# RWKV inverse in 16 by 16 blocks with its off-diagonal blocks on TensorE, new step weights, casts with priority, and another order in a sum of squares

## The chip, the cores and the metric

The kernel runs on one core of one Trainium2 chip. The metric is the device time of one execution in microseconds: before the change the median of 3 runs is 1454.53 us (1451.75 to 1456.83).

## The reference

Two layers (DEPTH = 2) over 256 tokens of width 1024, all in float32. Each layer is a half-step SwiGLU network, a mixer of three parallel branches, and a second half-step SwiGLU network. The mixer's branches are differential attention, RWKV-7 and HGRN2, all fed by one projection `u @ w_in`. The part that matters here is the RWKV recurrence, per head (8 heads, 64 by 64 state), one token after another:

```python
s_kk  = state @ kk_t
state = state * w_t - s_kk (x) (kk_t * a_t) + v_t (x) k_t
out_t = state @ r_t
```

and the normalisation ahead of each sub-layer, `y = x * rsqrt(mean(x*x) + eps) * w`, which needs the sum of squares of the residual stream over its 1024 channels.

## The kernel before, in words

**Weights.** All matrix products run on TensorE with every weight and activation split in two parts (high and low, type fp32r), three matmuls for each product (`mm3`, lines 363 to 369; the token-major form is lines 953 to 955). A weight tile is 128 by 1024 and takes 24 matmuls of 256 columns or 12 of 512. `load` (line 1339) fetches it into `raw` by a DMA on SP's queue; `split` (line 371) makes the high part `wh` by a cast on ScalarE (line 372) and the low part `wl` by a subtraction on VectorE (line 373). There are 4 `raw`, 3 `wh` and 3 `wl` buffers, and the program loads two tiles ahead of the one it multiplies.

**The order of the work.** The weights of one layer are a list of items; `ORDER` (line 52) is the mixer's part of it. Before the products of an item, `advance` (line 283) gives the other work a credit (`BUDGET`: 1.5 to 2.4 for an item in the stretch in question) and lets the side tracks take steps until it is spent. A step is a piece of a Python generator up to its `yield`; the yielded number is its price, and a negative one also ends the track's turn for this item. Tracks in the mixer are R (RWKV), H (HGRN2, `levels`), A, S0 and S1 (attention). What is emitted this way is then put in order for each engine, when the program is built, by a planner that goes by priority (earlier emitted is higher) and by its own costs; `ahead(n)` (line 266) moves a piece n places up. The engines run their instructions strictly in the order so found.

**The RWKV inverse.** Tokens are cut in chunks of 64, 4 chunks and 8 heads, so 32 triangular 64 by 64 matrices A for each layer. `rwkv_rest` (line 774) needs the inverse of I + A for each. Before the change it is built from 32 by 32 blocks:

- The two diagonal blocks of each matrix (64 blocks) go through DRAM (`scr`, lines 783 and 789) into a layout with one block per partition; they lie there twice, so 128 partitions are filled.
- A loop over t = 1 to 15 (lines 798 to 803) finds row t of the inverse of both 16 by 16 diagonal blocks of each block by a product (line 800) and a reduction (line 802) on VectorE, over 2 t t elements.
- The off-diagonal 16 by 16 block is then two products and two reductions over 2048 elements, also on VectorE (lines 809, 812, 814, 817), with copies around them (lines 806, 807, 819, 820).
- The result goes back through DRAM (`scy`, lines 822 to 824 and 828) into `Ys`, where the rows of a matrix lie on the partitions.
- The off-diagonal 32 by 32 block is made on TensorE: a transpose on VectorE (line 838), 32 products of 32 by 32 for each half p (line 842), a copy on ScalarE (844), 32 more products (848) and a copy into `Ys` on VectorE (850). For a given p all products of a series use the same 32 by 32 tile of the array.

After it the scan over 4 chunks follows (lines 854 to 903), then the head's normalisation and output gate.

`levels` (line 996) waits until `M["inv"]` is set by `rwkv_rest`, and its buffers `hw`, `sc01` and `sc2` lie where `TM`, `NT` and `Y` lay. `a_open` (line 1115) drains R before the attention starts.

**The sum of squares.** For each of 8 residual tiles, `z_square` (line 412) squares on ScalarE; the first makes `acc`, tiles 1 to 6 are added to it on GpSimd (line 419), and the last stays in `sq`. `z_sums` (line 426) sums both over partitions by matmuls with ones into one PSUM tile, `acc` first. It is emitted with a priority 584 places up.

Of the kernel before, what the change touches and what calls it, by code (L numbers as in the profile page):

```python
# [63 lines left out]
def trunk(ctx: ExitStack, tc: tile.TileContext, A, out):  # L64
# [192 lines left out]
    NOW = {}  # L257
# [292 lines left out]
    scr = drp.tile([2, 2, 16, 32, 32], F32, name="scrA")  # L550
    scy = drp.tile([2, 2, 16, 32, 32], F32, name="scrY")
# [3 lines left out]
    def mixer(l):  # L555
# [218 lines left out]
        def rwkv_rest():  # L774
# [5 lines left out]
            for q in range(2):  # L780
                for p in range(2):
                    r0 = 64 * p + 32 * q
                    GP.dma_start(scr[q, p].rearrange("m s t -> s m t"),
                                 H[r0:r0 + 32, :, :, 32 * q:32 * q + 32].rearrange("s j c t -> s (j c) t"))
            NT = tile_([128, 32, 32], "NT", "r")
            Y = tile_([128, 32, 32], "Y", "k")
            TM = hp.tile([128, 2048], F32, name="TM", tag="ZH")
            for d in range(2):
                GP.dma_start(NT[64 * d:64 * d + 64], scr.rearrange("q p m s t -> (q p m) s t"))
            GP.memset(Y, 0.0)  # L790
            GP.memset(Y.rearrange("m a b -> m (a b)")[:, 0:1024:33], 1.0)
# [6 lines left out]
            for t in range(1, 16):  # L798
                tm = TM[:, 0:2 * t * t].rearrange("m (g j s) -> m g j s", g=2, j=t)
                V.tensor_tensor(tm, ap(Y, 0, [[528, 2], [32, t], [1, t]]), ap(NT, t, [[528, 2], [0, t], [32, t]]),  # L800
                                ALU.mult)
                V.tensor_reduce(ap(Y, t, [[528, 2], [32, t]]), tm, AX.X, ALU.add)  # L802
                yield 0.2 + 4 * t * t / 960.0
            Yh = tile_([128, 8, 16], "Yh", "rnt")
            PT = tile_([128, 8, 16], "PT", "rny")
            V.tensor_copy(Yh[0:64], Y[0:64, 0:8, 0:16])
            V.tensor_copy(Yh[64:128], Y[64:128, 8:16, 0:16])
            tm = TM.rearrange("m (j t s) -> m j t s", j=8, t=16)
            V.tensor_tensor(tm, Yh.unsqueeze(2).to_broadcast([128, 8, 16, 16]),  # L809
                            ap(NT, 16, [[0, 8], [1, 16], [32, 16]]), ALU.mult)  # L810
            yield 2.2
            V.tensor_reduce(PT, tm, AX.X, ALU.add)
            yield 2.2
            V.tensor_tensor(tm, PT.unsqueeze(2).to_broadcast([128, 8, 16, 16]),  # L814
                            ap(Y, 528, [[0, 8], [1, 16], [32, 16]]), ALU.mult)
            yield 2.2
            V.tensor_reduce(Yh, tm, AX.X, ALU.add)
            yield -2.2
            V.tensor_copy(Y[0:64, 0:8, 16:32], Yh[0:64])
            V.tensor_copy(Y[64:128, 8:16, 16:32], Yh[64:128])  # L820
            sm = scy.rearrange("q p m s t -> (q p m) s t")
            GP.dma_start(sm[:, 0:8], Y[0:64, 0:8])
            GP.dma_start(sm[:, 8:16], Y[64:128, 8:16])
            GP.dma_start(sm[:, 16:32], Y[0:64, 16:32])
            for q in range(2):
                for p in range(2):
                    r0 = 64 * p + 32 * q
                    GP.dma_start(Ys[r0:r0 + 32, :, 32 * q:32 * q + 32], scy[q, p].rearrange("m s t -> s m t"))
            M["inv"] = True
            yield 0.255  # L830

            Xa = tile_([128, 16, 32], "Xa")
            Tt = tile_([128, 16, 32], "Tt")
            p1 = psm([128, 16, 32])
            p2 = psm([128, 16, 32])
            hv = [(slice(64 * p, 64 * p + 32), slice(64 * p + 32, 64 * p + 64)) for p in range(2)]
            for a_, b_ in hv:
                V.transpose(Xa[a_], Ys[a_, :, 0:32])
            yield -1.2
            for p, (a_, b_) in enumerate(hv):  # L840
                for m in range(16):
                    PE.matmul(p1[b_, m], H[a_, m // 4, m % 4, 32:64], Xa[a_, m], start=True, stop=True,
                              tile_position=(64 * p, 64 * p + 32))
                SC.copy(Tt[b_], p1[b_])
            yield -0.2
            for p, (a_, b_) in enumerate(hv):
                for m in range(16):
                    PE.matmul(p2[a_, m], Tt[b_, m], Ys[b_, m, 32:64], start=True, stop=True,
                              tile_position=(64 * p + 32, 64 * p))
# [489 lines left out]
    def load(i):  # L1339
# [5 lines left out]
        split(wh, wl, raw)  # L1345
# [125 lines left out]
```

## Time and profile before

| | before |
|---|---|
| median of 3 runs | 1454.53 us |
| the profiled execution's own time | 1448.06 us |
| its span, first to last instruction | 1446.4 us |
| TensorE busy (matmuls) | 1397.5 us, 97% |
| VectorE busy | 1185.8 us, 82% |
| ScalarE busy | 804.4 us, 56% |
| GpSimd busy | 149.0 us, 10% |

Busy time is the union of an engine's instructions. Matmuls are pipelined, so the number of matmuls that a stretch holds says more of TensorE's pace than its busy share does. The mixers lie at about 220 to 560 us (layer 0) and 925 to 1260 us (layer 1).

### The profile page before, as it was taken

How to read it: one execution, taken by the hardware profiler on the slowest of the kernel's cores; microseconds unless marked ns; L12 is line 12 of the kernel's file. 1: busy time of each engine (PE TensorE's matmuls, PEld its weight loads, DVE VectorE, ACT ScalarE, POOL GpSimd, SP SyncE). 2: the span in 40 equal slices, each digit the busy share in tenths (PEclk: the TensorE clock that was granted, in tenths of full speed). 3: DMA queues.
4: the chain of work that ended last, by engine and by line, in shares of the span. 5: the costliest groups of instructions: out<-in, count | busy, mean ns of one | idle time of the engine just before them, and what ended most of it. 6: DMA issues, size and time to landing. Idle time of an engine off the chain costs nothing. (4 is left out here: it accounts for less than half of the span.)

```text
span 1446.4 us, 31230 instructions
## 1 busy us (share of the span) xinstructions
PE 1397.5 (97%) x12424; PEld 1325.0 (92%) x12424; DVE 1185.8 (82%) x2216; ACT 804.4 (56%) x1375; POOL 149.0 (10%) x251
## 2 busy tenths in 40 slices
PE   4999999999899999999999999999989999999998
PEld 2899999998778999999999999999877889999998
DVE  5899988869779999888879888787797787886553
ACT  3565457874255646554555554588534664565542
POOL 6100010031310021000100000100322001100000
PEclk9999999999799999999999999999999999999999
DMA  9679985445416657899878998644552235665664
GB/s 334 247 267 359 341 303 167 148 155 163 137 61 191 203 190 265 298 330 319 297 255 292 353 347 294 194 141 142 180 162 83 88 129 175 198 220 194 193 197 124
DMA packets 90212, 315.99 MB, mean 218 GB/s; under 512 B 10577, under 2 KB 13009, under 8 KB 90066
## 3 DMA queue, kind: packets, MB, share of 16 engines
q1 hardware_dynamic: 86690, 308.32, 63.0%
q0 software_dynamic: 1600, 4.20, 1.2%
q8 instruction: 97, 1.59, 0.4%
q10 hardware_dynamic: 1776, 1.48, 0.3%
q14 instruction: 49, 0.40, 0.1%
HBM read 311.86 MB, written 2.10 MB: 217 GB/s over the span
## 5 line engine op out<-in xcount | busy, mean ns | idle before, releaser
L372 ACT CAST wh<-raw 128x1024 fp32r<-128x1024 f32 (+1 forms) x440 | 455.9, 1036 | 427.4 <-PE psd L369 241.5
L373 DVE TENSOR_TENSOR wl<-raw,wh 128x1024 fp32r<-128x1024 f32 (+1 forms) x440 | 537.2, 1222 | 109.1 <-ACT wh L372 106.2
L369 PE MATMUL psd<-uh,wl 128*128 128x256 f32 x1664 | 227.5, 278 | 6.2 <-DVE wl L373 6.2
L369 PE MATMUL psd<-uh,wh 128*128 128x256 f32 x1664 | 230.8, 280 | 0.0
L369 PE MATMUL psd<-ul,wh 128*128 128x256 f32 x1664 | 226.6, 278 | 0.0
L369 PEld LDWEIGHTS psd<-uh,wl 128*128 128x128 f32 x1664 | 206.0, 188 | 7.9 <-DVE wl L373 7.4
L369 PEld LDWEIGHTS psd<-uh,wh 128*128 128x128 f32 x1664 | 207.2, 188 | 5.0 <-issue 2.6
L369 PEld LDWEIGHTS psd<-ul,wh 128*128 128x128 f32 x1664 | 206.0, 188 | 0.4
L321 DVE SCALAR_TENSOR_TENSOR mw<-mw,cbc 128x1024 f32<-128x1024 f32 x134 | 168.0, 1256 | 0.0
L369 PE MATMUL psd<-hl,wh 128*128 128x256 f32 x704 | 96.0, 277 | 0.0
L369 PE MATMUL psd<-hh,wl 128*128 128x256 f32 x704 | 95.9, 277 | 0.0
L369 PE MATMUL psd<-hh,wh 128*128 128x256 f32 x704 | 95.5, 276 | 0.0
L419 POOL TENSOR_TENSOR acc<-acc,sq 128x256 f32<-128x256 f32 x36 | 31.4, 873 | 573.2 <-ACT sq L417 572.9
L369 PEld LDWEIGHTS psd<-hh,wl 128*128 128x128 f32 x704 | 87.2, 188 | 0.0
L369 PEld LDWEIGHTS psd<-hl,wh 128*128 128x128 f32 x704 | 87.2, 188 | 0.0
L369 PEld LDWEIGHTS psd<-hh,wh 128*128 128x128 f32 x704 | 87.0, 188 | 0.0
L954 PE MATMUL psd<-wl,uh 128*128 128x512 f32 x160 | 66.9, 418 | 3.9 <-DVE wl L373 3.8
L955 PE MATMUL psd<-wh,ul 128*128 128x512 f32 x160 | 67.7, 423 | 0.0
L953 PE MATMUL psd<-wh,uh 128*128 128x512 f32 x160 | 66.4, 416 | 0.0
L369 PE MATMUL psd<-zh,wh 128*128 128x258 f32 x448 | 65.2, 286 | 0.0
L369 PE MATMUL psd<-zh,wl 128*128 128x258 f32 x448 | 64.9, 283 | 0.0
L369 PE MATMUL psd<-zl,wh 128*128 128x258 f32 x448 | 64.0, 283 | 0.0
(430 smaller groups left out, 2032.0 us busy)
## 6 DMA issues: line engine op xcount, KB each, us to landing
raw<-in_gu SPq DMA_DIRECT2D x176, 512.0 KB, 4.7
mw<-in_modw SPq DMA_DIRECT2D x134, 512.0 KB, 5.4
raw<-in_wfm SPq DMA_DIRECT2D x94, 512.0 KB, 3.3
raw<-in_dn SPq DMA_DIRECT2D x64, 512.0 KB, 4.6
raw<-in_wtm SPq DMA_DIRECT2D x40, 512.0 KB, 3.3
raw<-in_dn SPq DMA_DIRECT2D x32, 384.0 KB, 4.1
raw<-in_wo SPq DMA_DIRECT2D x24, 512.0 KB, 3.3
raw<-in_wout SPq DMA_DIRECT2D x16, 512.0 KB, 3.3
```

The source lines that it names most:

```text
L321: ins = V.scalar_tensor_tensor(w, w, 1.0, NOW["cbc"], ALU.mult, ALU.mult, accum_out=modd[:, l, j, f:f + 1])
L369: PE.matmul(p, w[:, sl[k]], xs[k][x], start=first and i == 0, stop=last and i == 3 * n - 1)
L372: SC.copy(dst_h, src)
L373: V.tensor_sub(dst_l, src, dst_h.bitcast(F32))
L419: GP.tensor_add(NOW["acc"], NOW["acc"], sq)
L953: PE.matmul(ps[b], u[k][0][:, ts_], w1, start=k == 0, stop=False)
L954: PE.matmul(ps[b], u[k][0][:, ts_], w2, start=False, stop=False)
L955: PE.matmul(ps[b], u[k][1][:, ts_], w1, start=False, stop=k == KT - 1)
```

## The change

There are four parts.

1. The inverse starts from 16 by 16 blocks. The four diagonal blocks of each matrix (128 blocks) lie one per partition, not doubled, so the loop works on t t elements. The VectorE products for the off-diagonal 16 by 16 blocks and their copies go. The blocks come back through DRAM as the diagonal blocks of `Yd`; the off-diagonal 16 by 16 blocks are made on TensorE by two series of 64 products of 32 by 32, in which four tiles on the array's diagonal take turns, with a transpose on VectorE, a copy on ScalarE, an addition on VectorE, and copies into `Ys` by ScalarE and GpSimd. The two series for the 32 by 32 block follow, now with the two halves in turn. `Bd` holds the 16 by 16 blocks of A, copied on GpSimd.
2. The prices of the steps are others: a step of the loop takes `0.4 + 2.7 t t / 960` where it took `0.2 + 4 t t / 960`, and three steps of -0.1 stand after the DMAs.
3. The cast and the subtraction of each weight are emitted 100 places up in priority.
4. In `z_sums` the matmuls of `sq` come before those of `acc`.

```diff
-        for i, sq in enumerate((NOW["acc"], NOW["sq"])):
+        for i, sq in enumerate((NOW["sq"], NOW["acc"])):
...
+            quads = [(p, q, g, 64 * p + 32 * q) for p in range(2) for q in range(2) for g in range(2)]
+            for p, q, g, r in quads:
+                o = 32 * q + 16 * g
+                GP.dma_start(scr[p, q, g].rearrange("m s t -> s m t"),
+                             rows_(H[r + 16 * g:r + 16 * g + 16, :, :, o:o + 16]))
+            NT = tile_([128, 16, 16], "NT", "r")
+            Y = tile_([128, 16, 16], "Y", "k")
+            TM = tile_([128, 256], "TM", "rnt")
+            GP.dma_start(NT, scr.rearrange("p q g m s t -> (p q g m) s t"))
...
+            AI = tile_([128, 2, 16, 32], "AI", "a")
+            Bd, Yd = AI[:, 0], AI[:, 1]
+            GP.memset(AI, 0.0)
+            for p, q, g, r in quads:
+                if g == 0:
+                    GP.tensor_copy(Bd[r:r + 16, :, 16:32], rows_(H[r:r + 16, :, :, 32 * q + 16:32 * q + 32]))
...
             for t in range(1, 16):
+                tm = TM[:, 0:t * t].rearrange("m (j s) -> m j s", j=t)
+                V.tensor_tensor(tm, ap(Y, 0, [[16, t], [1, t]]), ap(NT, t, [[0, t], [16, t]]), ALU.mult)
+                V.tensor_reduce(ap(Y, t, [[16, t]]), tm, AX.X, ALU.add)
+                yield 0.4 + 2.7 * t * t / 960.0
+            GP.dma_start(scy.rearrange("p q g m s t -> (p q g m) s t"), Y)
+            for p, q, g, r in quads:
+                GP.dma_start(Yd[r + 16 * g:r + 16 * g + 16, :, 16 * g:16 * g + 16], scy[p, q, g].rearrange("m s t -> s m t"))
             M["inv"] = True
+            yield -0.1
+            yield -0.1
+            yield -0.1
...
+            V.transpose(Xa, Yd)
+            yield -0.6
+            for m in range(16):
+                for i, r in enumerate(quad):
+                    PE.matmul(p1[r, m], Bd[r, m], Xa[r, m], start=True, stop=True, tile_position=(32 * i, 32 * i))
+            SC.copy(Tt, p1)
+            yield -0.2
+            p2 = psm([128, 16, 32])
+            for m in range(16):
+                for i, r in enumerate(quad):
+                    PE.matmul(p2[r, m], Tt[r, m], Yd[r, m], start=True, stop=True, tile_position=(32 * i, 32 * i))
+            V.tensor_tensor(Yd[:, :, 16:32], Yd[:, :, 16:32], p2[:, :, 16:32], ALU.add)
+            for i, r in enumerate(quad):
+                (GP.tensor_copy if i % 2 else SC.copy)(Ys[r, :, 32 * (i % 2):32 * (i % 2) + 32], Yd[r])
+            V.transpose(Xa, Yd)
+            yield -1.0
...
-            for p, (a_, b_) in enumerate(hv):
-                for m in range(16):
+            for m in range(16):
+                for p, (a_, b_) in enumerate(hv):
                     PE.matmul(p1[b_, m], H[a_, m // 4, m % 4, 32:64], Xa[a_, m], start=True, stop=True,
                               tile_position=(64 * p, 64 * p + 32))
...
-        split(wh, wl, raw)
+        with ahead(100):
+            split(wh, wl, raw)
```

## Rows read from the trace of the kernel before

**Rows 1.** The page: busy times, and TensorE's busy tenths in 40 slices of 36 us.

```profile
PE 1397.5 (97%) x12424; PEld 1325.0 (92%) x12424; DVE 1185.8 (82%) x2216; ACT 804.4 (56%) x1375; POOL 149.0 (10%) x251
...
PE   4999999999899999999999999999989999999998
```

**Rows 2.** Busy time of each engine in stretches of 20 us (one of the dense feed-forward part, then the two inverses), and of 4 us around them. Columns: stretch, its length, then busy us and number of instructions for PE, PEld, DVE, ACT, POOL, then the granted clock, the DMA share and GB/s.

```profile
600.00:620.00 20.00, 20.00 (x178) 20.00 (x178) 17.47 (x27) 9.78 (x15) 0.00 (x0) 1.00 0.92 328
360.00:380.00 20.00, 15.61 (x99) 12.34 (x98) 17.74 (x17) 6.46 (x9) 8.36 (x12) 0.83 0.55 168
...
1060.00:1080.00 20.00, 14.90 (x88) 12.84 (x87) 19.94 (x15) 6.18 (x11) 7.48 (x11) 0.84 0.44 147
...
382.00:386.00 4.00, 4.00 (x116) 3.74 (x115) 1.00 (x2) 0.00 (x0) 0.25 (x1) 0.50 0.62 201
...
386.00:390.00 4.00, 4.00 (x24) 2.82 (x24) 2.43 (x5) 1.04 (x2) 0.52 (x1) 0.50 0.07 16
...
1074.00:1078.00 4.00, 3.50 (x8) 2.81 (x9) 3.94 (x8) 2.09 (x5) 2.17 (x5) 0.50 0.65 183
```

**Rows 3.** Whom TensorE's matmuls waited for over the whole span: total us, times, longest.

```profile
PE psd L369 <- DVE wl L373: 6.2, 6, 2.0
PE psm L430 <- POOL acc L419: 5.0, 5, 2.0
PE psd L954 <- DVE wl L373: 3.8, 2, 1.9
...
PE psm L750 <- ACT BK L742: 1.4, 2, 0.7
...
PE psm L848 <- issue: 0.5, 2, 0.3
```

**Rows 4.** VectorE in order of time, layer 1: start, length, line and form.

```profile
1057.61 4.07 DVE L809 TENSOR_TENSOR TM<-Yh,NT 128x2048 f32<-128x2048 f32 x1
...
1062.70 2.29 DVE L812 TENSOR_REDUCE PT<-TM 128x128 f32<-128x2048 f32 x1
...
1066.02 3.97 DVE L814 TENSOR_TENSOR TM<-PT,Y 128x2048 f32<-128x2048 f32 x1
...
1070.99 2.32 DVE L817 TENSOR_REDUCE Yh<-TM 128x128 f32<-128x2048 f32 x1
1073.19 1.26 DVE L373 TENSOR_TENSOR wl<-raw,wh 128x1024 fp32r<-128x1024 f32 x1
```

**Rows 5.** TensorE in order of time, layer 1 (start, length, line, form, how many; in brackets the idle time before and who ended it).

```profile
1071.17 1.19 PE L369 MATMUL psd<-uh,wl 128*128 128x256 f32 x8 [2.00 <-DVE wl L373]
...
1074.50 0.79 PE L954 MATMUL psd<-wl,uh 128*128 128x512 f32 x1 [1.91 <-DVE wl L373]
1075.09 0.63 PE L955 MATMUL psd<-wh,ul 128*128 128x512 f32 x1
1075.52 0.63 PE L953 MATMUL psd<-wh,uh 128*128 128x512 f32 x1
...
1080.86 0.40 PE L954 MATMUL psd<-wl,uh 128*128 128x512 f32 x1
1081.09 0.40 PE L955 MATMUL psd<-wh,ul 128*128 128x512 f32 x1
```

**Rows 6.** Small matmuls on TensorE in order of time: one tile of the array (L848 in layer 0, L842 and L848 in layer 1), four tiles in turn (L1017), and the first full-size matmul after such a series.

```profile
381.16 1.73 PE L848 MATMUL psm<-Ys,Tt 32*32 32x32 f32 x29
...
1083.26 1.19 PE L842 MATMUL psm<-Xa,H 32*32 32x32 f32 x32
1084.38 0.50 PE L955 MATMUL psd<-wh,ul 128*128 128x512 f32 x1
...
1086.54 1.08 PE L848 MATMUL psm<-Ys,Tt 32*32 32x32 f32 x29
...
1093.44 0.76 PE L1017 MATMUL psm<-hw 128*32 128x32 f32 x64
```

**Rows 7.** VectorE's loop in groups (line, operation, form, count, then busy us and mean ns): both layers, and its widest forms in layer 0.

```profile
L800 DVE TENSOR_TENSOR TM<-Y,NT 128x2 f32<-128x2 f32 (+14 forms) x30 | 15.4, 514 | 0.9
L802 DVE TENSOR_REDUCE Y<-TM 128x2 f32<-128x2 f32 (+14 forms) x30 | 9.7, 325 | 0.7
...
L800 DVE TENSOR_TENSOR TM<-Y,NT 128x450 f32<-128x450 f32 x1 | 1.0, 1006 | 0.0
```

**Rows 8.** GpSimd's DMA issues and VectorE's wait for them in layer 0, in order of time, and the medians from issue to landing of the kinds concerned (tile, queue, count, KB each, us).

```profile
374.23 2.60 POOL L828 DMA_DIRECT2D Ys<-scrY  x4 [0.34 <-issue]
...
379.20 0.70 DVE L838 STREAM_TRANSPOSE Xa<-Ys 32x512 f32<-32x512 f32 x1 [1.89 <-DMA Ys<-scrY]
...
Ys<-scrY POOLq DMA_DIRECT2D x8, 64.0 KB, 4.4
...
scrY<-Y POOLq DMA_DIRECT2D x2, 128.0 KB, 3.9
```

**Rows 9.** The sum of squares ahead of layer 0's second feed-forward part: TensorE, then ScalarE, in order of time.

```profile
556.22 0.61 PE L430 MATMUL psm<-ones,acc 128*128 128x1 f32 x4 [2.03 <-POOL acc L419]
...
559.42 0.61 PE L430 MATMUL psm<-ones,sq 128*128 128x1 f32 x4
...
558.97 0.40 ACT L417 ACTIVATE sq<-h 128x256 f32<-128x256 f32 x1
```

**Rows 10.** The casts of all weights in groups: busy us, mean ns, then idle time of the engine before them and what ended it.

```profile
L372 ACT CAST wh<-raw 128x1024 fp32r<-128x1024 f32 (+1 forms) x440 | 455.9, 1036 | 427.4 <-PE psd L369 241.5
```

More of the change, by code (lines that the diff above doesn't have):

```diff
@@ L547, in ffn @@
                 add(A["dn"][l, i, f][:, k0 * 128:(k0 + kn) * 128], kn * 128, partial(down, f, k0, kn))
-    scr = drp.tile([2, 2, 16, 32, 32], F32, name="scrA")
-    scy = drp.tile([2, 2, 16, 32, 32], F32, name="scrY")
+    scr = drp.tile([2, 2, 2, 16, 16, 16], F32, name="scrA")
+    scy = drp.tile([2, 2, 2, 16, 16, 16], F32, name="scrY")
     c3 = lambda t: t.rearrange("p (c t) -> p c t", t=C)
@@ L778, in rwkv_rest @@
                 GP.memset(Ys[64 * p + 32:64 * p + 64, :, 0:32], 0.0)
[L780 to L789, printed above, removed]
-            GP.memset(Y, 0.0)
-            GP.memset(Y.rearrange("m a b -> m (a b)")[:, 0:1024:33], 1.0)
+            quads = [(p, q, g, 64 * p + 32 * q) for p in range(2) for q in range(2) for g in range(2)]
+            rows_ = lambda t: t.rearrange("s j c t -> s (j c) t")
+            for p, q, g, r in quads:
[6 more added lines that the diff above has]
+            GP.dma_start(NT, scr.rearrange("p q g m s t -> (p q g m) s t"))
+            GP.memset(Y, 0.0)
+            GP.memset(Y.rearrange("m a b -> m (a b)")[:, 0:256:17], 1.0)
+            AI = tile_([128, 2, 16, 32], "AI", "a")
[4 more added lines that the diff above has]
+                    GP.tensor_copy(Bd[r:r + 16, :, 16:32], rows_(H[r:r + 16, :, :, 32 * q + 16:32 * q + 32]))
             yield 0.1
@@ L798, in rwkv_rest @@
             for t in range(1, 16):
[L799 to L828, printed above, removed]
+                tm = TM[:, 0:t * t].rearrange("m (j s) -> m j s", j=t)
@@ L829, in rwkv_rest @@
+                V.tensor_tensor(tm, ap(Y, 0, [[16, t], [1, t]]), ap(NT, t, [[0, t], [16, t]]), ALU.mult)
[4 more added lines that the diff above has]
+                GP.dma_start(Yd[r + 16 * g:r + 16 * g + 16, :, 16 * g:16 * g + 16], scy[p, q, g].rearrange("m s t -> s m t"))
             M["inv"] = True
-            yield 0.255
+            yield -0.1
@@ L832, in rwkv_rest @@
+            yield -0.1
+            yield -0.1
             Xa = tile_([128, 16, 32], "Xa")
             Tt = tile_([128, 16, 32], "Tt")
+            quad = [slice(32 * i, 32 * i + 32) for i in range(4)]
+            p1 = psm([128, 16, 32])
+            V.transpose(Xa, Yd)
[4 more added lines that the diff above has]
+            SC.copy(Tt, p1)
@@ L836, in rwkv_rest @@
             hv = [(slice(64 * p, 64 * p + 32), slice(64 * p + 32, 64 * p + 64)) for p in range(2)]
-            for a_, b_ in hv:
-                V.transpose(Xa[a_], Ys[a_, :, 0:32])
-            yield -1.2
-            for p, (a_, b_) in enumerate(hv):
-                for m in range(16):
+            for m in range(16):
+                for p, (a_, b_) in enumerate(hv):
                     PE.matmul(p1[b_, m], H[a_, m // 4, m % 4, 32:64], Xa[a_, m], start=True, stop=True,
                               tile_position=(64 * p, 64 * p + 32))
+            for p, (a_, b_) in enumerate(hv):
                 SC.copy(Tt[b_], p1[b_])
             yield -0.2
+            for m in range(16):
+                for p, (a_, b_) in enumerate(hv):
+                    PE.matmul(p2[a_, m], Tt[b_, m], Yd[b_, m], start=True, stop=True,
+                              tile_position=(64 * p + 32, 64 * p))
             for p, (a_, b_) in enumerate(hv):
-                for m in range(16):
-                    PE.matmul(p2[a_, m], Tt[b_, m], Ys[b_, m, 32:64], start=True, stop=True,
-                              tile_position=(64 * p + 32, 64 * p))
                 V.tensor_copy(Ys[a_, :, 32:64], p2[a_])
```

## The prediction, made before the change was run

> **What bounds the kernel now.** I read the page first. TensorE's matmuls are busy for 1397.5 us of 1446.4, VectorE for 1185.8, ScalarE for 804.4, and TensorE is full in nearly every slice but the first [rows 1]. So this is a kernel paced by TensorE: nothing that only makes VectorE lighter pays, unless TensorE was waiting for it. The stretches of time show where it was. A dense stretch of 20 us holds 178 matmuls with no gap; 360 to 380 us holds 15.61 us of work at a mean clock of 0.83, and 1060 to 1080 us holds 14.90 at 0.84, with VectorE busy for 17.74 and 19.94 us [rows 2]. Both are the end of the RWKV inverse. The list of waits says for what: 6.2 + 3.8 us for the low part of a weight (`wl`, VectorE), and 5.0 us for `acc` (GpSimd) [rows 3]. All eight waits for `wl` lie in these two stretches or just before them. VectorE in order of time shows why: the four wide instructions, 4.07, 2.29, 3.97 and 2.32 us, each stand ahead of a 1.2 us subtraction of a weight [rows 4], and TensorE starts when that ends.
>
> The two last gaps, of 2.00 and 1.91 us, have a second price. After them the 512-column matmuls of layer 1 come every 0.43 us, later every 0.23 [rows 5], and the granted clock is 0.50, the lower level of 1.2 GHz [rows 2]. In layer 0 the lower level returns at 382 to 390 us [rows 2], during the small matmuls of the old off-diagonal block; layer 1 at the same place stays at the full clock, as 29 small matmuls in 1.08 us against 1.73 us show [rows 6].
>
> **The change part by part.**
>
> *Inverse, what goes.* On VectorE 4.07 + 2.29 + 3.97 + 2.32 = 12.7 us of each layer [rows 4], and up to half of the loop, (15.4 + 9.7) / 2 = 12.6 us a layer [rows 7]. Its widest product takes 1.01 us for 450 elements while the mean of all is 0.51, so a part is fixed; I take 3.3 us between 0 and 6.3. That is 16 us of 128 partitions' work out of a stretch where VectorE was full. A weight needs 1.2 us of VectorE [rows 4] in the 2.7 us of its 24 matmuls (24 / 178 of 20 us [rows 2]), so with no instruction over some 1.2 us left in the way `wl` is in time. I count all of the waits for it: **-10.0 us** (6.2 + 3.8). If other side work were packed just as densely into the freed time, this would be 0.
>
> *The clock after these waits.* In layer 1 the slow spacing lasts from 1074.5 to about 1080.2 us, 13 matmuls at 0.20 us too much, 2.6 us [rows 5]. The same in layer 0, read off a mean clock of 0.83 in 20 us: 3.4 us of clock missing, of which the part outside the idle time is about 2.1. Together **-4.7 us**, if the gaps go. The second low stretch in layer 0, at least 8 us at half rate, is worth between 0 and 4 us; the small matmuls stay and their number doubles, so I take less than half: **-1.5 us**.
>
> *Inverse, what comes.* 128 more matmuls of 32 by 32 in a layer. The lower bound is a series over four tiles in turn, 64 in 0.76 us, or 12 ns each; the upper is one tile, 32 in 1.19 us, or 37 ns [rows 6]: 1.5 to 4.7 us. The new series do use four tiles in turn, so I take 1.5. The old 128 now alternate between two tiles; they took about 32 x 4 x 36 ns = 4.6 us and may keep that or fall to half; I take 0.7 less. A full-size matmul right after a small series takes 0.50 us where one in a row takes 0.40 [rows 5, 6]; four more such changes are 0.4 us. A layer comes to 1.5 - 0.7 + 0.4 = 1.2, both to **+2.4 us**, between -1.6 and +10.
>
> The Trainium skill bears on this twice, and speaks against the change. "TensorEngine Tiling (Array Packing)", section Key Properties, says that a change of tiling mode drains TensorE; the 0.1 us above is what it costs here. "TensorE: Matmul & The Clock Gate", section "Wait — 56ns, not 53.3ns?", says that matmuls never start closer than about 25 ns however small they are; by that, as an estimate, 256 new ones take 6.4 us instead of 3.0 and the sum below is 3.4 us worse. The 64 in 0.76 us disagree with it [rows 6], and I go by the row.
>
> *The chain of the inverse.* After the loop there is one store, 8 loads issued by GpSimd instead of 4, a transpose, and four series on TensorE with copies between them instead of two. An issue takes 0.65 us (4 in 2.60), so 8 take 5.2; the store lands after 3.9 us and a load 4.4 us after its issue [rows 8]: 3.9 + 0.65 + 5.2 + 4.4 - 0.65 = 13.5 us from loop to transpose, where before the transpose stood idle for the last 1.89 us [rows 8]. Three steps of -0.1 and the transpose's turn spread this over about four weights, 4 x 2.7 = 11 us, so the transpose may sit for 2 to 3 us at the head of VectorE's queue with weights' subtractions behind it. TensorE has one or two weights ready, 2.7 to 5.4 us, which covers it; without cover it costs 2 to 3 us a layer. The 8 loads on the way in cost 2.6 us more of GpSimd's issue, and `AI`'s fill and the copies into `Bd` and `Ys` come to GpSimd too, which is busy for 149 us of 1446 [rows 1]; this delays the start of the loop and the level sums of H, for which no matmul of a weight waits. Before, eight half series lost 0.5 us on TensorE, and eight full ones will lose as much; I add **+0.8 us**, bounds -0.5 and +6.
>
> *Step prices.* The yields of the loop summed to 15 x 0.2 + 4 x 1240 / 960 = 8.2, and 8.8 for the four wide steps, 17.0 in all; now 15 x 0.4 + 2.7 x 1240 / 960 = 9.5. At a budget of 2.0 the inverse is emitted over about 5 weights instead of 8.5. H's levels may then start some 4 weights sooner. The scan, by my count of the credits, is emitted about 2 weights later, but already before the change it ran as late as its inputs, not as its emission: 0.
>
> *Priority of casts.* ScalarE's casts already wait 427 us for buffers, 241 of them for TensorE [rows 10]: they stand at the head of a queue until TensorE releases `wh`. Being planned earlier can't make that release earlier. It can end waits like the 0.7 us for `BK` [rows 3] or lengthen them by one cast of 1.04 us each. Bounds: -3 us, and +13 for a dozen such waits. I take 0.
>
> *The sum of squares.* TensorE reaches `acc` too early, five times, 5.0 us; the matmuls of `sq` stand 3 us later and start when ScalarE has just ended `sq` (559.42 after 558.97 + 0.40) without a wait [rows 3, 9]. With `sq` first, the group can't begin before that, and `acc` is long there: **-5.0 us**. What it costs is that `acc`'s four matmuls, some 0.45 us, now lie between `sq` and the chain for `rstd`; at most 5 x 0.45 = 2.3 us, and I take **+0.5**, since other products can fill it.
>
> **Sum.** -10.0 - 4.7 - 1.5 + 2.4 + 0.8 - 5.0 + 0.5 = -17.5 us, from 1448.06 us of the profiled execution (span 1446.4 and 1.7 around it) to 1430.6. That execution was 6.5 us quicker than the median of the runs; none of my terms depends on that, so I take the same step from the median: 1454.5 - 17.5 = **1437 us**. All favourable ends together give -10 - 4.7 - 4 - 1.6 - 0.5 - 3 - 5 = -29, 1426 us; the unfavourable ones with the waits for `wl` still gone give -10 + 10 + 6 + 13 - 2.7 = +16.
>
> **Rivals.**
> 1. *All goes well, and more*: the second low stretch of the clock goes too, the alternating tiles halve the old series, and the priority ends waits elsewhere. The other waits of the list, `BK`'s with 0.7 us the longest of those shown [rows 3], are short, so there is little to win: 1426 us. Chance 0.10.
> 2. *The wait is replaced.* VectorE is as full as before, since H's five narrow levels now fall on the same weights, and the transposes wait for their DMA at the head of the queue; the clock drops as before. For it: VectorE has no idle time in 1060 to 1080. Against it: after the change no part of the inverse on VectorE is longer than the subtraction of a weight. Then only `acc` is won, against 2.4 + 0.8 + 0.5: 1453 us. Chance 0.13.
> 3. *Slower: casts ahead of evacuations.* With 100 places of priority a cast is planned ahead of an evacuation of PSUM, but on the chip its buffer comes later than planned; ScalarE, which runs in order, stands at the cast and the evacuation behind it, and TensorE runs out of PSUM. It decides once an evacuation is later than the four PSUM buffers allow, about two weights or 5.4 us. The price is about one cast, 1.04 us, each time [rows 10]. At 17 of the 440 weights it has eaten the 17.5 us; with 25 of them the time is 1454.5 - 17.5 + 26 = 1463 us. For it: ScalarE's idle time lies before these casts. Against it: the dense stretches have no gap at all and VectorE has 2.5 us of 20 spare there. Chance 0.11.
>
> **How the numbers follow.** My forecast of 1437 us has 0.66; its own range is 1427 to 1447. A change under 0.3%, or 4.4 us, is one that a measurement of this kernel can't tell from none. Rival 2, at 1453, is within that for most of its spread. Faster: 0.66 + 0.10 and a little of rival 2, 0.78; the same: 0.11; slower: 0.11. The range that leaves out two in ten reaches from the good end to about where rival 2 lies: 1424 to 1453.
>
> **What would show it.** In the profile after: no wait of a matmul for `wl` of more than a few tenths in either inverse, VectorE no longer full there, the granted clock 1.00 in 20 us stretches around the inverse (0.83 and 0.84 now), `acc` gone from the list of TensorE's waits, and 64 small matmuls of a new series in about 0.8 us. The prediction fails if TensorE's waits for `wl` remain or new ones on the transposes or the copies take their place, or if the feed-forward parts, untouched but for the casts' priority, hold fewer than 178 matmuls in 20 us.

## The result, and the profile after

The changed kernel takes 1464.5 us (median of 4 runs, 1462.8 to 1467.0), the kernel before 1454.7 us beside it: a ratio of 1.0069, with a 95% interval from 1.0046 to 1.0091. The forecast was 1437 us; the change made the kernel slower by 10 us.

The page of the profiled execution (span 1462.5 us; compare [rows 1]): TensorE's busy time, its busy tenths in 40 slices, and the queue that brings the engines their instructions (packets, MB, share).

```profile
PE 1400.1 (96%) x12936; PEld 1328.9 (91%) x12936; DVE 1158.4 (79%) x2202; ACT 804.9 (55%) x1381; POOL 168.2 (12%) x275
...
PE   4999999997999999999999999999979999999998
...
q8 instruction: 102, 1.67, 0.5%
```

VectorE is 27 us lighter over both layers (the prediction counted 16 a layer), and GpSimd 19 us busier. TensorE executes 512 matmul instructions more, and its idle time, the span less the busy time, has risen from 48.9 to 62.4 us. Around either inverse one slice holds a 7 where one held an 8.

The stretches there, of the changed kernel (columns as in [rows 2], which has 0.83 and 0.84 for the clock at the inverses):

```profile
360.00:380.00 20.00, 15.80 (x545) 14.59 (x546) 10.56 (x13) 6.71 (x11) 4.73 (x6) 0.63 0.13 43
...
1070.00:1090.00 20.00, 11.46 (x463) 10.47 (x464) 7.52 (x10) 4.94 (x9) 3.06 (x4) 0.61 0.18 63
600.00:620.00 20.00, 20.00 (x179) 20.00 (x178) 17.64 (x27) 10.83 (x16) 0.00 (x0) 1.00 0.88 299
```

The dense part is as it was (179 matmuls against 178), so the loss isn't there. At the inverses VectorE is no longer full (10.56 and 7.52 us of 20 against 17.74 and 19.94), and yet TensorE has gaps and the granted clock is lower than before. VectorE, GpSimd and the DMA engines have become idle together with TensorE: a sign that they stand behind one thing.

Whom TensorE's matmuls waited for in the changed kernel (total us, times, longest; compare [rows 3]):

```profile
PE psm L825 <- DVE Xa L821: 12.5, 2, 6.3
...
PE psd L957 <- DVE wl L373: 4.7, 5, 1.8
PE psm L831 <- issue: 3.6, 2, 2.4
PE psm L1020 <- issue: 2.9, 2, 1.7
...
PE psm L750 <- ACT BK L742: 2.2, 5, 0.7
```

The waits for `acc` and those of L369 for `wl` have gone, 5.0 and 6.2 us. In their place TensorE stands for 6 us per layer at the first new series (L825), for the transposed blocks, and for 1.2 to 2.4 us at a time with no wait at all ("issue"). The next view shows both: TensorE in order of time, layer 0, changed kernel.

```profile
354.76 0.63 PE L369 MATMUL psd<-uh,wh 128*128 128x256 f32 x4
361.57 1.93 PE L825 MATMUL psm<-Xa,AI 32*32 32x32 f32 x128 [6.18 <-DVE Xa L821]
363.44 1.08 PE L1020 MATMUL psm<-hw 128*32 128x32 f32 x64
364.45 0.68 PE L831 MATMUL psm<-AI,Tt 32*32 32x32 f32 x40
366.32 0.95 PE L831 MATMUL psm<-AI,Tt 32*32 32x32 f32 x88 [1.19 <-issue]
367.20 0.39 PE L369 MATMUL psd<-uh,wh 128*128 128x256 f32 x1
367.77 0.68 PE L1020 MATMUL psm<-hw 128*32 128x32 f32 x38 [0.19 <-DVE hw L1071]
369.70 0.59 PE L1020 MATMUL psm<-hw 128*32 128x32 f32 x26 [1.25 <-issue]
```

TensorE breaks off inside a weight (four matmuls of a group of eight, 354.76) and stands at L825 until 361.57. The other matmuls of the group use the same high part, so they are ready, but they come later in its order. From the store of the loop's result (349.15 us, below) to this place it had executed 52 matmuls of weights, 2.2 weights in 6 us. After the gap the clock is low (0.63 in the mean of this stretch): 64 matmuls of L1020 take 1.08 us, where such a series took 0.76 before [rows 6]. Then it stops in the middle of L831, after 40 of 128, where the profile shows nothing that it waits for.

The wait comes from the round trip through DRAM. VectorE's longest waits for DMA, and GpSimd in order of time, changed kernel:

```profile
DVE Xa L821 <- DMA AI<-scrY: 12.1, 2, 6.1
...
DVE TM L807 <- DMA NT<-scrA: 8.4, 2, 4.2
```

```profile
318.21 4.52 POOL L785 DMA_DIRECT2D scrA<-H  x8 [3.17 <-DVE H L755]
322.73 3.24 POOL L798 COPY AI<-H 16x256 f32<-16x256 f32 x4
...
327.17 2.34 POOL L1081 TENSOR_TENSOR PX<-PX 128x512 f32<-128x512 f32 x1
329.45 0.59 POOL L790 DMA_DIRECT2D NT<-scrA  x1
...
349.15 0.60 POOL L810 DMA_DIRECT2D scrY<-Y  x1
351.48 4.49 POOL L812 DMA_DIRECT2D AI<-scrY  x8 [1.73 <-DMA scrY<-Y]
```

From the end of the eight stores to the load of `NT` pass 6.7 us, filled with other work of GpSimd, and the loop's first instruction holds VectorE's queue for 4.2 us. From the store of the result at 349.15 to the transpose at 360.81 pass 11.7 us.

### The profile page after: what moved, and what is told of

Same layout as the page of the kernel before. It is cut to its first block, busy times and chain, and to the rows that moved or that the text cites. A ratio compares the mean times of both kernels' runs of the same rounds, so it can differ in the third digit from the quotient of the medians.

```text
span 1462.5 us, 32284 instructions
## 1 busy us (share of the span) xinstructions
PE 1400.1 (96%) x12936; PEld 1328.9 (91%) x12936; DVE 1158.4 (79%) x2202; ACT 804.9 (55%) x1381; POOL 168.2 (12%) x275
## 3 DMA queue, kind: packets, MB, share of 16 engines
q1 hardware_dynamic: 86690, 308.32, 62.4%
q8 instruction: 102, 1.67, 0.5%
## 4 chain that ended last, share of the span: by engine, by line
PE 78%; DVE 10%; ACT 4%; DMA 3%; POOL 3%; issue 2%; DVEq 0%; ACTq 0%; POOLq 0%; SPq 0%
PE psd L369 66%; DVE wl L373 3%; ACT wh L372 1%; PE psd L956 1%; PE psd L957 1%; PE psd L958 1%; DVE mw L321 1%; DMA AI<-scrY 1%; DMA raw<-in_wfm 1%; POOL scrA L785 1%; PE psm L750 1%; DVE TM L807 1%; PE psm L1020 1%; POOL AI L812 1%; PE psm L676 0%
## 5 line engine op out<-in xcount | busy, mean ns | idle before, releaser
L369 PE MATMUL psd<-uh,wh 128*128 128x256 f32 x1664 | 235.1, 281 | 0.0
L369 PE MATMUL psd<-ul,wh 128*128 128x256 f32 x1664 | 229.7, 279 | 0.0
L369 PE MATMUL psd<-uh,wl 128*128 128x256 f32 x1664 | 229.1, 279 | 0.0
L369 PEld LDWEIGHTS psd<-uh,wh 128*128 128x128 f32 x1664 | 208.9, 189 | 6.3 <-issue 4.0
L369 PEld LDWEIGHTS psd<-uh,wl 128*128 128x128 f32 x1664 | 207.6, 189 | 1.0 <-issue 0.7
L369 PEld LDWEIGHTS psd<-ul,wh 128*128 128x128 f32 x1664 | 207.7, 189 | 0.8
L419 POOL TENSOR_TENSOR acc<-acc,sq 128x256 f32<-128x256 f32 x36 | 35.3, 980 | 569.3 <-ACT sq L417 433.3
L369 PE MATMUL psd<-hl,wh 128*128 128x256 f32 x704 | 95.4, 276 | 0.0
L369 PE MATMUL psd<-hh,wh 128*128 128x256 f32 x704 | 95.4, 276 | 0.0
L369 PE MATMUL psd<-hh,wl 128*128 128x256 f32 x704 | 95.4, 276 | 0.0
L369 PEld LDWEIGHTS psd<-hl,wh 128*128 128x128 f32 x704 | 86.9, 188 | 0.0
L369 PEld LDWEIGHTS psd<-hh,wh 128*128 128x128 f32 x704 | 86.9, 188 | 0.0
L369 PEld LDWEIGHTS psd<-hh,wl 128*128 128x128 f32 x704 | 86.9, 188 | 0.0
L957 PE MATMUL psd<-wl,uh 128*128 128x512 f32 x160 | 64.9, 405 | 5.0 <-DVE wl L373 4.7
L369 PE MATMUL psd<-zh,wh 128*128 128x258 f32 x448 | 65.3, 286 | 0.0
L369 PE MATMUL psd<-zh,wl 128*128 128x258 f32 x448 | 64.9, 284 | 0.0
L369 PE MATMUL psd<-zl,wh 128*128 128x258 f32 x448 | 63.9, 283 | 0.0
L958 PE MATMUL psd<-wh,ul 128*128 128x512 f32 x160 | 63.9, 399 | 0.0
```

The source lines that it names most:

```text
L369: PE.matmul(p, w[:, sl[k]], xs[k][x], start=first and i == 0, stop=last and i == 3 * n - 1)
L419: GP.tensor_add(NOW["acc"], NOW["acc"], sq)
L957: PE.matmul(ps[b], u[k][0][:, ts_], w2, start=False, stop=False)
L958: PE.matmul(ps[b], u[k][1][:, ts_], w1, start=False, stop=k == KT - 1)
```

## The experiments

Ratios are to the kernel before, run beside each; 0.0010 of it is 1.45 us. Theory A: the round trips through DRAM stand at the head of TensorE's and VectorE's queues. Theory B: the casts' priority is what the change loses by.

**One part each.** The order of the z sum alone, the priority alone, and the inverse with its steps alone, each put into the kernel before.

```diff
-        for i, sq in enumerate((NOW["acc"], NOW["sq"])):
+        for i, sq in enumerate((NOW["sq"], NOW["acc"])):
```

> The kernel before with one edit: the matmuls of the last square come before those of acc. If the reordered sum is worth what the two traces suggest (five joints where the changed kernel gains 1.2 to 2.1 us each), this takes 5 to 9 us off 1454.7, and acc leaves the list of TensorE's waits. If the later start of the chain for rstd eats it, it is within 2 us of before.

```diff
-        split(wh, wl, raw)
+        with ahead(100):
+            split(wh, wl, raw)
```

> The kernel before with one edit: cast and subtraction of a weight 100 places up. Theory A (the slow-down is the inverse's wait for its DMA): within 3 us of before. Theory B (the casts' priority delays evacuations and the steps of the tracks): 8 to 14 us slower, with the loss in the first third of the mixers and in the attention, none in the feed-forward parts.

The third is the changed kernel with these two edits undone.

> The changed kernel with the sum's order and the casts' priority put back: the new inverse and its step prices alone. Theory A: 12 to 20 us slower than before, since the first series of small matmuls stands 6 us a layer at the head of TensorE's queue. Theory B: 0 to 6 us slower.

Measured: the z sum 0.9952 (0.9935 to 0.9970), 1446.7 us, so -7 us; the priority 1.0137 (1.0114 to 1.0160), +20 us; the inverse 1.0096 (1.0079 to 1.0113), +14 us. Together that would be +27 us, and the change is +10: the priority and the inverse overlap. The inverse came out as theory A had it (12 to 20 us). The priority alone fits neither theory: 3 us at most by A, 8 to 14 by B.

**More steps ahead of the transpose.** The changed kernel with eight steps of -0.1 instead of three.

```diff
-            yield -0.1
-            yield -0.1
+            for _ in range(7):
+                yield -0.1
             yield -0.1
```

> The changed kernel with eight steps of -0.1 after the DMAs instead of three; nothing is left out. In TensorE's order the first series then stands 2.8 weights, 7.6 us, later. Theory A: the waits of 6.2 us a layer and the lower clock after them go, 15 to 25 us faster than the changed kernel, about 1440 to 1450. Theory B: under 5 us faster.

Measured 1.0073 (1.0052 to 1.0094): no gain. TensorE's list of waits of this run no longer has L825, but this:

```profile
PE psm L1020 <- DVE hw L1066: 5.4, 2, 2.7
...
PE psm L1055 <- issue: 3.4, 2, 1.9
```

So the wait of 12.5 us could be taken away and the time stayed; theory A's 15 to 25 us did not come. TensorE is idle for 62.8 us in this run, against 62.4. The stall without a wait is now at L1055, and by the same list H's level sums (L1020, 7.1 us in all, 0.2 in the changed kernel) and the recurrence (L868 to L900, 5.5 us, not in the changed kernel's list) wait for what begins later.

**Without the priority; without the loads; with half of the new products.**

```diff
-        with ahead(100):
-            split(wh, wl, raw)
+        split(wh, wl, raw)
```

> The changed kernel without the casts' priority: the z sum's order, the new inverse and its three steps stay. Theory A (the inverse's DMA round trips stand at the head of TensorE's and VectorE's queues; the casts' priority costs little besides): TensorE still waits about 6 us per layer for the transposed blocks, and the time stays between 1460 and 1466 us. Theory B (the casts' priority, which alone cost 18 us, is what the changed kernel loses by): the small series of the mixers' front come back to the spans of the kernel before, about 3.4 us per layer and as much again in the rest of the layer, and the time falls to between 1446 and 1455 us.

```diff
             for p, q, g, r in quads:
-                GP.dma_start(Yd[r + 16 * g:r + 16 * g + 16, :, 16 * g:16 * g + 16], scy[p, q, g].rearrange("m s t -> s m t"))
+                pass
```

> The changed kernel, but the eight loads that bring the diagonal blocks back from DRAM are left out (the blocks keep their zeros, so the inverse is not the reference's). Theory A: TensorE's wait for the transposed blocks goes, and with it the stretch at half clock behind it, 6 + 3 us per layer: the time falls by 12 to 18 us, to 1447 to 1453 us. Theory B: the wait goes, but the casts' priority keeps its cost: the time falls by under 8 us.

```diff
-            for m in range(16):
+            for m in range(8):
                 for i, r in enumerate(quad):
...
-            SC.copy(Tt, p1)
+            SC.copy(Tt[:, 0:8], p1[:, 0:8])
...
-            V.tensor_tensor(Yd[:, :, 16:32], Yd[:, :, 16:32], p2[:, :, 16:32], ALU.add)
+            V.tensor_tensor(Yd[:, 0:8, 16:32], Yd[:, 0:8, 16:32], p2[:, 0:8, 16:32], ALU.add)
```

> The changed kernel with the off-diagonal blocks of 8 instead of 16 of the inverse's columns of blocks computed (half of the 256 new small matmul instructions per layer are left out, the rest of the inverse is as it was; the output is not the reference's). If TensorE's stalls without any wait (1.2 to 2.4 us behind the dense small series) come from the number of instructions that it has to be given, the stalls behind the two new series fall from 3.6 + 2.9 us to under 3 us in all and the time falls by 3 to 6 us; if they are something else, both stay within 1 us, and the time falls by about 2 us, the busy time of the matmuls left out.

Measured: without the priority 1.0048 (1.0032 to 1.0064), 1461.4 us, 3 us less than the changed kernel by the ratios, which their intervals don't tell from none; so theory B does not explain the result. (It is 7 us less than the inverse alone, from which it differs by the z sum: the same -7 us.) Without the loads 0.9936 (0.9921 to 0.9951), 19 us less, a little more than theory A's 18. But more than the wait went with the loads: the stalls without a wait fell from 6.5 to 2.1 us, and the granted clock is 1.00 around both inverses, so the 19 us are not the price of the wait alone. And with half of the new products 0.9989 (0.9978 to 1.0000), 12 us less, twice what I had expected at most, though the instructions left out are worth only 3 to 4 us of busy time (256 at 12 to 15 ns). TensorE's waits in that run:

```profile
PE psm L825 <- DVE Xa L821: 12.3, 2, 6.3
...
PE psm L1020 <- issue: 0.6, 1, 0.6
```

The wait for the blocks is untouched, the stalls without a wait have fallen from 6.5 us to 0.6. This speaks for a price of the number of instructions in a dense series: theory D, that TensorE uses up its instructions and stands until more have come.

**Six steps, and GpSimd's copies later.** The kernel without the priority, with six steps ahead of the transpose and the copies into `Bd` written into the loop's sixth step.

```diff
-            for p, q, g, r in quads:
-                if g == 0:
-                    GP.tensor_copy(Bd[r:r + 16, :, 16:32], rows_(H[r:r + 16, :, :, 32 * q + 16:32 * q + 32]))
             yield 0.1
...
                 V.tensor_reduce(ap(Y, t, [[16, t]]), tm, AX.X, ALU.add)
+                if t == 6:
+                    for p, q, g, r in quads:
+                        if g == 0:
+                            GP.tensor_copy(Bd[r:r + 16, :, 16:32], rows_(H[r:r + 16, :, :, 32 * q + 16:32 * q + 32]))
...
-            yield -0.1
-            yield -0.1
-            yield -0.1
+            for _ in range(6):
+                yield -0.1
```

> Without the casts' priority; GpSimd's four copies of the off-diagonal blocks stand after the load of the loop's operand instead of ahead of it (in the loop's sixth step), and six steps instead of three lie between the loop and the transpose. Theory A: VectorE's wait for the loop's operand (4.2 us) falls to under 1.5 us, TensorE's wait for the transposed blocks (6.2 us) to under 1 us, and the time is 10 to 16 us under the run without the priority alone. Theory C (a wait that is taken away at one place is given back at the next, since the time is set by what follows: the recurrence and the waits of the gates behind it): the two waits go as well, but the time differs from that run by less than 4 us.

Measured 1.0008 (0.9996 to 1.0019), 6 us under the run without the priority: less than theory A's 10, more than theory C's 4. Only one of the two waits went. TensorE no longer waits at L825. VectorE's wait is as before, 4.2 us per layer: in the trace the copies still stand ahead of the load on GpSimd (319.81 and 326.37 us), whatever their place in the code. So this run tells of the six steps, not of the copies. The stalls remain, in TensorE's list of this run and, layer 0, in order of time:

```profile
PE psm L831 <- issue: 4.9, 2, 2.8
PE psm L1020 <- DVE hw L1066: 4.6, 2, 2.3
```

```profile
365.60 1.49 PE L831 MATMUL psm<-AI,Tt 32*32 32x32 f32 x125
369.23 0.25 PE L831 MATMUL psm<-AI,Tt 32*32 32x32 f32 x3 [2.15 <-issue]
```

A low clock is not what makes them: in this run the granted clock is 1.00 from 358 to 370 us, and 125 matmuls take 1.49 us, 12 ns each, before the stall. The clock falls after it, to 0.57 in 370 to 374 us.

**The same number of instructions, spread out.** The last kernel, with each new series cut in two halves.

```diff
             for m in range(16):
+                if m == 8:
+                    yield -0.1
                 for i, r in enumerate(quad):
                     PE.matmul(p1[r, m], Bd[r, m], Xa[r, m], start=True, stop=True, tile_position=(32 * i, 32 * i))
...
             for m in range(16):
+                if m == 8:
+                    yield -0.1
                 for i, r in enumerate(quad):
                     PE.matmul(p2[r, m], Tt[r, m], Yd[r, m], start=True, stop=True, tile_position=(32 * i, 32 * i))
```

> The kernel of the run nt_first, with each of the two new series of 128 small matmul instructions cut in two halves of 64 with a step of the plan between them, so that matmuls of weights stand between the halves. Nothing is left out. Theory D (TensorE uses up its instructions in a dense series of more than about 170 small ones and then stands until more have come): the stalls without a wait behind the second series, 2.1 and 2.8 us in nt_first, fall under 1 us each, though the number of instructions is the same, and the time falls by 3 to 6 us, to 1449 to 1452 us. Theory C (what is won there is lost at the recurrence and the gates, which begin one to two weights later): the stalls go, but the time stays within 2 us of nt_first's 1455 us.

Measured 1445.3 us, 0.9932 (0.9914 to 0.9951): 11 us under nt_first, about twice what was expected, with nothing left out. No row of TensorE's list names "issue" any more. The stretches of this run, and TensorE in order of time:

```profile
360.00:380.00 20.00, 20.00 (x520) 18.42 (x508) 16.53 (x20) 15.80 (x30) 5.93 (x6) 1.00 0.50 153
...
1070.00:1090.00 20.00, 20.00 (x520) 18.18 (x506) 15.70 (x19) 14.68 (x30) 5.02 (x6) 1.00 0.46 149
```

```profile
358.69 0.75 PE L827 MATMUL psm<-Xa,AI 32*32 32x32 f32 x64
...
363.01 0.75 PE L827 MATMUL psm<-Xa,AI 32*32 32x32 f32 x64
...
367.32 0.75 PE L835 MATMUL psm<-AI,Tt 32*32 32x32 f32 x64
```

TensorE is full in these stretches, the clock is 1.00 in both, and 64 instructions take 0.75 us. The same edit alone in the changed kernel:

> The changed kernel with one edit: each of the two new series of 128 small matmul instructions is cut into two halves of 64 with a step of the plan between them. The casts' priority and the three steps stay. Theory D (the instructions of a dense series run out): the stalls without a wait (3.6 + 2.9 us) go, TensorE's wait for the transposed blocks (12.5 us) stays, and the time falls by 5 to 10 us, to 1454 to 1460 us. Theory A (the wait for the transposed blocks alone is what counts): the time stays within 3 us of the changed kernel's 1464.5 us.

Measured 1.0010 (0.9992 to 1.0029), 1457.3 us: 8.6 us of the changed kernel's loss by the difference of the ratios. The wait for the transposed blocks is still there (12.7 us); the stalls without a wait have fallen from 6.5 to 1.1 us, and the clock comes back sooner. One stretch of the changed kernel, then of this run:

```profile
370.00:374.00 4.00, 4.00 (x92) 3.65 (x82) 1.15 (x2) 1.03 (x2) 0.19 (x1) 0.50 0.02 6
370.00:374.00 4.00, 4.00 (x150) 3.70 (x149) 3.97 (x6) 1.80 (x4) 1.20 (x3) 1.00 0.12 22
```

In the changed kernel the clock is at the lower level from 370 to 378 us, here it is 1.00 from 366 us on. So the stalls cost twice: their own time, and matmuls at a lower clock behind them (as in nt_first, above).

**The price of the priority.** The kernel spread with the priority put back; then with the priority everywhere but in the fronts of the mixers, and there alone.

> The kernel of the run spread (1445.3 us) with the casts' priority of the changed kernel put back. Theory B (the priority has a price of its own, in the mixers' front, where the small series wait for ScalarE's copies): it is slower by 5 to 9 us, 1450 to 1455 us, about 3.4 us of it in the front of each layer's mixer. If the priority's price is hidden by other waits as it nearly was in the changed kernel, the time is within 3 us of spread's; if it is as in the kernel before (cast_only), it is slower by about 18 us.

```diff
-        with ahead(100):
+        with ahead(0 if NOW.get("front") else 100):
             split(wh, wl, raw)
```

> The kernel of the run spread_ahead, in which the casts' priority cost 12 us against spread, with the priority switched off in the front of each mixer alone (from the norm of the keys to the start of the inverse) and kept everywhere else. If the price is the casts that ScalarE is given ahead of the copies of BK in the front, 3.4 us and more per layer, the fronts come back to 84 and 99.7 us as in spread and the time falls by 6 to 12 us, to 1445 to 1451 us. If the price lies in the attention part and the feed-forward part, the fronts come back, but the time stays over 1453 us.

> The opposite of rest_ahead: the priority in the front of each mixer alone. If the front is the place of the price, TensorE's waits for BK return and the time lies 7 us or more over spread's 1445.3 us, at 1452 to 1457 us; if the place is elsewhere, it is within 4 us of spread's.

Measured: everywhere 1.0017 (1.0001 to 1.0033), 12 us over spread, more than the 5 to 9 expected; everywhere but in the fronts 0.9965 (0.9947 to 0.9984), 5 us over, just within the noise; in the fronts alone 0.9996 (0.9982 to 1.0010), 9 us over. So most of it lies in the fronts. ScalarE there, in the changed kernel and then in the run no_ahead:

```profile
258.63 1.03 ACT L372 CAST wh<-raw 128x1024 fp32r<-128x1024 f32 x1
...
259.97 1.05 ACT L372 CAST wh<-raw 128x1024 fp32r<-128x1024 f32 x1
...
262.00 0.41 ACT L742 COPY BK<-k 64x256 f32<-64x256 f32 x1
```

```profile
258.53 1.05 ACT L372 CAST wh<-raw 128x1024 fp32r<-128x1024 f32 x1
...
260.03 0.41 ACT L742 COPY BK<-k 64x256 f32<-64x256 f32 x1
```

With the priority a second cast stands ahead of the copies into `BK`; the copy of L742 comes 2 us later, and with it the products of L750, at 262.46 instead of 260.49 us. TensorE's own waits for `BK` hardly change by it (1.4 us in rest_ahead, 1.9 in front_ahead); it is the chain that gets longer. The first square of the keys (ScalarE, L662) and the first store of the inverse's blocks (GpSimd, L785) mark a front's two ends, here in layer 0 of rest_ahead and then of front_ahead:

```profile
236.80 0.51 ACT L662 ACTIVATE KS<-kk,cols 128x256 f32<-128x256 f32 x1
315.15 4.51 POOL L785 DMA_DIRECT2D scrA<-H  x8 [3.17 <-DVE H L755]
```

```profile
236.24 0.51 ACT L662 ACTIVATE KS<-kk,cols 128x256 f32<-128x256 f32 x1
317.60 4.51 POOL L785 DMA_DIRECT2D scrA<-H  x8 [3.16 <-DVE H L755]
```

That is 78.4 us against 81.4. In either layer a front takes 78.2 to 78.4 us without the priority (the kernel before, no_ahead, spread, rest_ahead) and 81.2 to 82.8 with it (the changed kernel, cast_only, spread_ahead, front_ahead): 3 us or more a layer, some 6 of the 9 us. What lies outside the fronts was not followed up: 5 us here, and in the kernel before some 14 of the priority's 20.

Spread_ahead also prices the wait for the transposed blocks. It differs from after_halves by the six steps and the later copies, and the 12.7 us of waiting are gone from its list; yet the two runs, 1457.3 us each, take the same time. So with the priority in place that wait was worth nothing, as in pace8; without it (nt_first against no_ahead) it was worth 6 us at most.

**The other way to get at the waits for `wl`.** The kernel z_only, with each of the old inverse's four wide instructions cut into two halves with steps between (one of the four is shown).

```diff
-            V.tensor_reduce(PT, tm, AX.X, ALU.add)
-            yield 2.2
+            for h in halves:
+                V.tensor_reduce(PT[:, h], tm[:, h], AX.X, ALU.add)
+                yield 1.1
```

> The kernel before with the z sum's order of the changed one (as z_only), the old inverse and casts, and each of the inverse's four wide VectorE operations (4.0, 2.3, 3.9 and 2.3 us) cut into two halves with steps between, so that the low halves of a weight can pass between them; no DMA and no matmul is added. If the wide operations in front of the low halves are what TensorE's 10 us of waits for them come from, as the prediction said, these waits fall to under 4 us, and the time is 4 to 8 us under z_only's 1446.7 us. If the low halves stand behind something else (the raw weights, ScalarE's high halves), the waits stay over 7 us and the time within 2 us of z_only's.

Measured 1444.6 us, 0.9927 (0.9908 to 0.9946), 3.6 us under z_only by the ratios, which the intervals don't tell from none. The expectation on the waits was wrong: the planner put the eight halves side by side, and TensorE waits once per layer, longer, in this run's list:

```profile
PE psd L369 <- DVE wl L373: 16.8, 2, 8.4
```

TensorE waits more for `wl` in total (17.4 us against 10.4 in z_only) and the time is no longer. A sum of waits is no measure of time; why the longer waits cost nothing here was not found.

## Why the prediction was wrong

Two readings failed, and both went into one term of the sum, +0.8 us for the chain of the inverse.

- *"eight half series lost 0.5 us on TensorE, and eight full ones will lose as much".* This is the step whose price the runs show. The series lost 6.5 us in stalls without a wait, and with the lower clock behind them that is 9 to 12 us of time (after_halves 8.6, spread 11; half_small 12, of which 3 to 4 are busy time left out). Spreading the same instructions out takes it away.
- *The transpose "may sit for 2 to 3 us", and "TensorE has one or two weights ready, 2.7 to 5.4 us, which covers it".* The chain itself was sized well (13.5 us; 11.7 measured), but three steps did not spread it over "about four weights", 11 us: TensorE was at the first new series after 2.2 weights, 6 us. It runs in order too, so the weights were ready but behind that series, and it stood for 6.2 us a layer. The prediction named new waits on the transposes as a sign of its failing. What this wait cost by itself is less clear: nothing where it was removed with the priority in place (pace8, spread_ahead), at most 6 us without.
- *The clock, -4.7 and -1.5.* These counted on the waits' going. The clock fell instead, to 0.63 and 0.61 in 20 us at the inverses, and is 1.00 there in spread, where neither that wait nor the stalls are left.
- *"128 more matmuls of 32 by 32 in a layer".* A product of two float32 blocks is two instructions in the trace, so a layer got 256; at 12 ns these are 3.1 us, where I had counted 1.5. The old 128 made up for it by luck: with two tiles in turn 64 of them take 1.20 us at the full clock (L847 and L854 of spread), so they took 2.2 us less and not 0.7.
- *Priority of casts: "I take 0", between -3 and +13.* It costs 3 us in the changed kernel (within the noise), 12 once the waits and stalls are mended and 20 in the kernel before, above my upper bound. Rival 3 came near the mechanism, a cast in ScalarE's order ahead of something that TensorE needs, but I argued against it from the dense stretches; where its place was found, in the mixers' fronts, it acts at copies and not at PSUM's evacuations. That Rival 3's 1463 us is near the measured time is luck.
- *GpSimd's extra work delays the loop, "for which no matmul of a weight waits".* VectorE stood 4.2 us per layer at the loop's first instruction, with subtractions of weights queued behind it, and TensorE waited 1.3 us a layer for one of these (at 335.54 us in layer 0). Of the 10.0 us of its waits for `wl`, of which I had counted all as won, 4.7 us are left (L957).
- *The z sum, -5.0 + 0.5.* Right in direction and a little small: -7 us.
- *The waits for `wl`.* Those of L369 went as I had said. What I had not asked is what comes late next. Rival 2 (*the wait is replaced*) named it, with the transposes at the head of a queue, but took VectorE's queue for the one that mattered, and its 1453 us were 11 too few.

So of the gain in sight only the z sum came. The new inverse, spread out and without the priority, ends at 1445.3 us (0.9932), where z_only with the old inverse has 1446.7 (0.9952), a difference within the noise. The list of the run spread suggests where the rest went:

```profile
PE psm L1024 <- DVE hw L1070: 4.7, 2, 2.3
PE psd L961 <- DVE wl L373: 3.6, 4, 1.4
```

The waits for `wl` have fallen from z_only's 10.4 us to 3.6, but TensorE now waits for H's level sums (L1024, 6.4 us in all) and the recurrence (L872 to L904, 5.2 us), which together stood for 0.4 us in z_only; its idle time is 51.2 us against 50.2. The lighter VectorE bought next to nothing. What beats both kernels here is the order of the z sum, alone or with either of the two mended inverses.

## What to carry to other kernels

When work is taken from one engine and given to a chain of DMA and small matmuls on the engine that sets the pace, look at the place in that engine's own order where the chain's first instruction stands: what is ready behind it covers nothing. Count small matmuls as instructions and lay wide ones between them. Give a priority only after looking at what the same engine must do in time for others, and test the parts of a change singly and together, since their costs hide each other. Don't price a wait by its length: here waits of 12.7 us could be taken away for nothing, because other waits took their place.

## What the runs showed of the hardware

TensorE seems to run out of instructions. In layer 0 of the changed kernel it executed 88 + 1 + 38 = 127 matmul instructions between one stall and the next (366.32 to 369.70 us, the view above); in layer 1, at the same place, it did as many:

```profile
1080.48 0.97 PE L831 MATMUL psm<-AI,Tt 32*32 32x32 f32 x91 [2.38 <-issue]
1081.38 0.58 PE L369 MATMUL psd<-uh,wh 128*128 128x256 f32 x1
1081.89 0.74 PE L1020 MATMUL psm<-hw 128*32 128x32 f32 x35
1084.33 0.65 PE L1020 MATMUL psm<-hw 128*32 128x32 f32 x29 [1.69 <-issue]
```

91 + 1 + 35 is 127 again. Each has a weight load beside it (the page counts as many PEld as PE), so 254 instructions lie between two stalls, and from one resumption to the next pass 3.4 us in layer 0 and 3.9 us in layer 1. The instruction queue of the profile moves 1.67 MB in 102 packets, 16.4 KB each; in the kernel before it is this:

```profile
q8 instruction: 97, 1.59, 0.4%
```

512 matmuls and 512 weight loads more are 1024 instructions, and the packets are 4 more in most runs of the new inverse (101), 5 in the changed kernel's: about 256 of TensorE's instructions to a packet, by these counts. The Trainium skill, "Runtime: NRT & Kernel Launch", section "Instruction fetch mechanics", says that an engine's instructions are fetched in blocks of 16 KiB, 256 instructions. Size and count agree with the rows. That page of the Trainium skill calls the cost of crossing from one block to the next mostly hidden; if the stalls are these crossings, it was not here, with 127 matmuls used up in 2.1 us. That the stalls are these fetches is inferred from the counts; that the density of the instructions makes them is shown by half_small, spread and after_halves. How long a dense series may be was not settled: the 170 of an expectation is in no run, and behind the long wait 192 small matmuls pass without a stall in half_small.

Small matmuls themselves went quicker than the floor of the Trainium skill that is named in the prediction ("TensorE: Matmul & The Clock Gate", section "Wait — 56ns, not 53.3ns?", about 25 ns): 64 in 0.75 us in the run spread, 12 ns each, with four tiles of the array in turn. With two tiles in turn it is 19 ns (64 in 1.20 us), with one 37 ns (32 in 1.19 us, [rows 6]).
